# A fixed order and a window for the first loads of an encoder kernel, and tables loaded later

## The chip, the cores and the metric

The kernel runs on one core of a Trainium2 chip. The metric is the device time of one execution in microseconds; lower is better. The core has TensorE (PE, with its weight loads PEld), VectorE (DVE), ScalarE (ACT), GpSimd (POOL) and SyncE (SP). SP issues the loads here, and 16 DMA engines carry them out.

## The reference, cut to what matters

One encoder block in float32, 256 tokens of width 2048. The first projection of the input is where the change lies:

```
x (1, 256, 2048); w_in (2048, 2624)
proj = x @ w_in                       # split: q_a 1024, k_a 256, v_a 256, c_q 512, c_kv 512, k_r 64
q_a, k_a = rope(rms_norm(q_a, g_qa)), rope(rms_norm(k_a, g_ka))      # 8 and 2 heads of 128
o_a = attention(q_a, k_a, v_a)
q_b, kv_b = rms_norm(c_q, g_cq) @ w_uq, rms_norm(c_kv, g_ckv) @ w_ukv
o_b = attention(q_b with rope, kv_b and rope(k_r))
x = LN1(alpha*x + [o_a, o_b] @ w_out)
x = LN2(alpha*x + cross_attention(x, LNm(mem)))
x = LN3(alpha*x + relu(x @ w1)**2 @ w2)
```

## The kernel before

Every float32 matmul is made of three fast ones: a number is split into a rounded part (hi, an ACT copy to a rounded type) and a rest (lo, a DVE subtraction), and `mm3` multiplies hi by hi, hi by lo and lo by hi. `split` (lines 87 and 88) makes the two parts for inputs and weights alike.

Weights come through `Stream`. A stream reads tiles of up to 1 MB (128 partitions by 2048 numbers) into `raw`, of which there are three buffers, and hands out halves split into `w_hi` and `w_lo`. The load of a tile waits until the tile three before it has been split. The first group of queries, `q_group(0, prologue, 4)`, reads its four tiles finely (`fine=4`): each tile in four pieces of 512 columns, one piece for each k of the contraction (16 in all), at line 150. Ahead of each such piece `load_x` may load the part of the transposed input that this k needs (line 254): one k for k = 0 and 1, then two k together for each even k. So the program's order is x0, w0, x1, w1, x2 (for k = 2 and 3), w2, w3, x4, w4, w5, and so on. All other tiles are loaded whole, at line 152.

`proj_tokens` runs over k and, for each k, over the two blocks of 128 tokens: six matmuls for a k, adding up in two PSUM tiles `acc`. The streams in order are: w_qa's first four tiles (queries 0 to 3), w_ka (two tiles), w_vkr (four tiles of 640 KB), attention of four heads, then w_qa's other four tiles, then w_ckv and w_cq for the second attention. `qk_heads` normalizes and rotates the heads, with tables `tab` that POOL multiplies together at line 265.

Two helpers load small tables. `load_tables` (lines 258 to 260) loads the rotation tables and gains for q_a, k_a and k_r, and is called by `prologue` when k is 14, ahead of x14, w14 and w15. `load_more` (lines 268 to 271) loads the gains of the two latents, the rotation table for q_b and the rows for the later norms; the program has it between w_ka and w_vkr.

Before all this, `busy(8)` issues eight matmuls on a tile of ones.

The order of instructions on each engine is set by a planner when the program is built: it simulates a timeline and takes, on each engine, what is ready first by priority. It can thus move a load ahead of one that stands before it in the program. `queue` pins an order by hand: it adds an edge from each instruction given to it to the one before on the same engine. The stages of the MLP, far later, use it for PE, ACT and DVE. Loads are not pinned in the kernel before. Every load also uses one of a few semaphores in turn, and SP waits until the former load on that semaphore has landed.

Of the kernel before, what the change touches and what calls it, by code (L numbers as in the profile page):

```python
# [18 lines left out]
P = 128  # L19
S = 256  # L20
D = 2048
KT = D // P
# [16 lines left out]
def encoder_kernel(ctx: ExitStack, tc: tile.TileContext, t, out):  # L39
    nc = tc.nc  # L40
# [26 lines left out]
    def att_tile():  # L67
        return psT.tile([P, 512], F32, tag="att", name="att")

    def tmp_tile():  # L70
        return rings["tmp"].tile([P, 512], F32, tag="tmp", name="tmp")

    def lo_tile():
        if fixed_lo:
            fixed_lo.rotate(-1)
            return fixed_lo[-1]
        return rings["lo"].tile([P, 1024], F32R, tag="w_lo", name="w_lo")

    def raw_tile():
        return rawp.tile([P, 2048], F32, tag="raw", name="raw")  # L80
# [24 lines left out]
    def queue(ins):  # L105

        i = ins.ins
        if i.engine in queued:
            tc.add_manual_dep(i, queued[i.engine], mybir.DependencyInfo(
                mybir.DependencyClass.NoSync, mybir.DependencyReason.DATA), reason="queue")  # L110
        queued[i.engine] = i.name
        return ins

    def pump(n=1):

        for _ in range(n):
            if banks or side:
                (banks or side).popleft()()
# [4 lines left out]
    def busy(n):  # L123

        ps = acc_tile()
        for _ in range(n):
            tc.keep_in_program_order(
                nc.tensor.matmul(ps, ones, ones[:, None, :].broadcast_to([P, 4, P]),
                                 start=True, stop=True))

    busy(8)

    class Stream:


# [4 lines left out]
        def next(self, hi=None, lo=None):  # L140
            u, h = divmod(self.n, 2)
            size = self.ap.shape[2]
            w = size // 2
            if h == 0:
                self.raw = raw_tile()
            g = w // 2 if u < self.fine else w
            if u < self.fine:
                for i, o in enumerate(range(h * w, h * w + w, g)):
                    self.before(4 * u + 2 * h + i)
                    nc.sync.dma_start(self.raw[:, o:o + g], self.ap[u][:, o:o + g])  # L150
            elif h == 0:
                nc.sync.dma_start(self.raw[:, :size], self.ap[u])
            self.n += 1
            if hi is None:
                hi = wsp.tile([P, 1024], F32R, tag="w_hi", name="w_hi")
                lo = lo_tile()
            for o in range(0, w, g):
                self.split(hi[:, o:o + g], lo[:, o:o + g], self.raw[:, h * w + o:h * w + o + g],
                      pinned=self.pinned)
            pump(self.beside)  # L160
            return hi[:, :w], lo[:, :w]
# [7 lines left out]
    def proj_tokens(stream, xt, nk, cols, before=None, by_block=None, wide=None, tiles=None):  # L169


        ps = [(tiles or acc_tile)() for _ in range(NB + bool(by_block))]
        parts, k = [], 0
        while k < nk:
            if before is not None:
                before(k)
            hi, lo = stream.next() if wide is None else wide(k)
            kk = hi.shape[1] // cols
            hi = hi.rearrange("p (k c) -> p k c", c=cols)
            lo = lo.rearrange("p (k c) -> p k c", c=cols)  # L180
            parts.append([(k + j, hi[:, j, :], lo[:, j, :]) for j in range(kk)])
            k += kk
            if not by_block:
                tokens_mm(ps, xt, parts.pop(), nk, 0, cols, range(NB))
        if by_block:
            half = cols // 2
            pieces = [(0, 0, cols, ps[0]), (1, 0, half, ps[1]), (1, half, half, ps[2])]
            for b, c, w, p_ in pieces:
                for part in parts:
                    tokens_mm({b: p_}, xt, part, nk, c, w, [b])  # L190
        else:
            pieces = [(b, 0, cols, ps[b]) for b in range(NB)]
        return pieces if by_block is not None else ps

    def tokens_mm(ps, xt, part, nk, c, w, blocks):
        for k, hi, lo in part:
            for b in blocks:
                o = b * P
                mm3(ps[b][:, :w], xt[:, k, o:o + P], xt[:, k, S + o:S + o + P],
                    hi[:, c:c + w], lo[:, c:c + w], k == 0, k == nk - 1)  # L200
# [23 lines left out]
    def transpose_split(dst, src, k0, b, nk=4, width=P):  # L224

        ps = att_tile()
        for j in range(nk):
            nc.tensor.transpose(ps[:, j * P:(j + 1) * P], src[:, j * P:(j + 1) * P], ident)
        o = b * P
        v = ps[:, :nk * P].rearrange("p (k c) -> p k c", c=P)  # L230
        split(dst[:, k0:k0 + nk, o:o + P], dst[:, k0:k0 + nk, S + o:S + o + P], v)
# [4 lines left out]
    gcq, gckv = tab_a[:, 0:512], tab_a[:, 512:1024]  # L236
    tab = tab_a[:, 1024:2048].rearrange("p (i b c) -> p i b c", i=4, b=NB)
    cs_n, gr = tab_b[:, 0:512], tab_b[:, 512:1024]
    krt = tab_b[:, 1536:1792].rearrange("p (i b c) -> p i b c", i=2, b=NB)
    qrt = midp.tile([P, 2, S], F32, name="qrt")  # L240
    gbt = const.tile([P, 3, 2, KT], F32, name="gbt")
# [3 lines left out]
    xt = xt_t.rearrange("p (k c) -> p k c", c=512)  # L245
    x_raw = big.tile([P, 8192], F32, tag="big", name="x_raw")

    def load_x(k):

        n = 1 if k < 2 else 0 if k % 2 else 2  # L250
        if not n:
            return
        src = x_raw[:, k * S:(k + n) * S]
        nc.sync.dma_start(src, t["xT"][k // 4][:, (k % 4) * S:(k % 4 + n) * S])
        split(xt[:, k:k + n, 0:S], xt[:, k:k + n, S:2 * S], src.rearrange("p (k c) -> p k c", c=S))

    def load_tables():
        nc.sync.dma_start(cs_n, t["rope_a"])
        nc.sync.dma_start(gr, t["g_qk"].partition_broadcast(P))
        nc.sync.dma_start(krt, t["rope_kr"])  # L260
        for i in range(4):
            cs = cs_n[:, (i % 2) * 256:(i % 2) * 256 + 256].rearrange("p (b d) -> p b d", b=NB)
            g = gr[:, i * DH:(i + 1) * DH]
            for b in range(NB):
                nc.gpsimd.tensor_tensor(out=tab[:, i, b, :], in0=cs[:, b, :], in1=g, op=ALU.mult)

    def load_more():
        nc.sync.dma_start(gckv, t["g_ckv"].partition_broadcast(P))
        nc.sync.dma_start(gcq, t["g_cq"].partition_broadcast(P))
        nc.sync.dma_start(qrt, t["rope_qr"])  # L270
        nc.sync.dma_start(gbt, t["norm_rows"])

    attA = big.tile([P, 8192], F32R, tag="big", name="attA")
    qa = attA[:, 0:4096].rearrange("p (h c) -> p h c", c=512)
# [170 lines left out]
                  lambda st: (va[:, st, g * P:(g + 1) * P], va[:, st, 256 + g * P:256 + (g + 1) * P]),  # L445
                  ot, h)

    def q_group(g4, before=None, fine=0):
        stream = Stream(t["w_qa"][g4 * 4:g4 * 4 + 4], fine)
        stream.before = load_x  # L450
        ps = proj_tokens(stream, xt, KT, 512, before)
        for b in range(NB):
            qk_heads(ps[b], b, 4, tab[:, 0, b, :], tab[:, 1, b, :], qa, g4 * 4, SC_A)

    def prologue(k):
        if k == 14:
            load_tables()

    q_group(0, prologue, 4)
    ps = proj_tokens(Stream(t["w_ka"]), xt, KT, KVA * DH)  # L460
    for b in range(NB):
        qk_heads(ps[b], b, KVA, tab[:, 2, b, :], tab[:, 3, b, :], ka, 0)
    load_more()
    ps = proj_tokens(Stream(t["w_vkr"]), xt, KT, KVA * DH + ROPE)
    for b in range(NB):
        split(va[:, b, 0:256], va[:, b, 256:512], ps[b][:, 0:256])
        krn = tmp_tile()
        v = ps[b][:, 256:256 + ROPE]
        a, c, e = krn[:, 0:64], krn[:, 64:128], krn[:, 256:384]
        nc.vector.tensor_tensor(out=a, in0=v, in1=krt[:, 0, b, :], op=ALU.mult)  # L470
        for i in range(2):
            j = 1 - i
            nc.vector.tensor_tensor(out=c[:, i * 32:(i + 1) * 32], in0=v[:, j * 32:(j + 1) * 32],
                                    in1=krt[:, 1, b, i * 32:(i + 1) * 32], op=ALU.mult)
        nc.vector.tensor_tensor(
            out=e.rearrange("p (g c) -> p g c", g=2), in0=a[:, None, :].broadcast_to([P, 2, ROPE]),
            in1=c[:, None, :].broadcast_to([P, 2, ROPE]), op=ALU.add)
        transpose_split(kr, e, 0, b, nk=1)
    heads = Heads()
    for h in range(4):  # L480
        heads.step(gqa_head(h))
# [21 lines left out]
    for n in range(2):  # L503
        ps = proj_tokens(s_vb, ckv, RANK // P, 512)
# [186 lines left out]
    ps = proj_tokens(Stream(t["w_vm"]), memt, KT, 512)  # L691
# [18 lines left out]
    for n in range(2):  # L710
        ps = proj_tokens(s_om, om, HM, 512)
# [203 lines left out]
    for c, q in PASSES:  # L915
# [3 lines left out]
        for u in us:  # L919
            n = 2 if q == 0 and u[3] == (CH // 2 - 2 if c else 0) else 1  # L920
# [462 lines left out]
```

## Time and profile before

| what | value |
|---|---|
| median of 3 runs | 1097.58 us |
| lowest and highest run | 1096.8 and 1098.6 us |
| the profiled execution's own time | 1098.32 us |
| its span, first to last instruction | 1096.5 us |
| mean granted TensorE clock | 0.996 |
| TensorE busy | 1076.7 us (98%) |
| VectorE busy | 938.7 us (86%) |
| ScalarE busy | 642.3 us (59%) |
| mean DMA rate over the span | 197 GB/s |

The span is what the trace shows; the rest of the execution's time lies around it. In the rows below, L150 is line 150 of the kernel, PE acc L164 a matmul of that line into the tile acc, and `w_hi<-raw` means that w_hi is written from raw. "SPq" rows are loads issued by SP; their duration is that of the issue, not of the transfer. "x2" merges two neighbours of one kind. A bracket at the end of a row is the engine's idle time before it and what ended it.

### The profile page before, as it was taken

Reading aid. Unit: us, or ns where it says so; the run is one execution under the profiler, and the core shown is the slowest. Engines: PE = TensorE matmul, PEld = TensorE weight load, DVE = VectorE, ACT = ScalarE, POOL = GpSimd, SP = SyncE. Lnnn points to the kernel's source line nnn. Section 1 sums busy time; section 2 is a strip of 40 time slices with the busy share of each in tenths; the row PEclk is TensorE's granted clock in tenths of the full one; section 3 lists DMA queues with packets and bytes.
Section 4 is the critical chain, followed back from the end, with each engine's and each line's share of the span. In section 5 each row is a group of like instructions: output and inputs, shape, how many; then the busy total and the mean of one; then the engine's idle time right before and its main releaser. Section 6 shows DMA issues by size and latency. Waiting matters only on the chain.

```text
span 1096.5 us, 15253 instructions
## 1 busy us (share of the span) xinstructions
PE 1076.7 (98%) x5846; PEld 928.8 (85%) x5846; DVE 938.7 (86%) x1301; ACT 642.3 (59%) x937; POOL 36.2 (3%) x43
## 2 busy tenths in 40 slices
PE   9999999999999999999999999999999999999995
PEld 6988899988999878878888888888888888888885
DVE  6878678778889677999999999899999899999876
ACT  6555567555576426656566557466566566666640
POOL 2402000000000000000000000000000000000000
PEclk9999999999999999999999999999999999999998
DMA  9664454466577334555556555646556555655732
GB/s 327 246 227 136 156 189 157 156 228 238 182 216 267 143 128 176 209 192 198 191 202 244 202 188 199 216 170 226 198 186 225 198 192 198 224 175 195 253 145 78
DMA packets 37369, 215.87 MB, mean 197 GB/s; under 512 B 4272, under 2 KB 5168, under 8 KB 13616
## 3 DMA queue, kind: packets, MB, share of 16 engines
q1 hardware_dynamic: 37296, 214.89, 55.5%
q8 instruction: 46, 0.75, 0.3%
q14 instruction: 27, 0.22, 0.1%
HBM read 212.78 MB, written 2.10 MB: 196 GB/s over the span
## 4 chain that ended last, share of the span: by engine, by line
PE 92%; DVE 6%; issue 1%; ACT 1%; DMA 1%; SPq 0%; POOL 0%; DVEq 0%; ACTq 0%
PE acc L164 12%; PE acc L165 12%; PE acc L166 12%; PE acc L1035 11%; PE att L1035 6%; PE acc L1043 6%; PE att L165 5%; PE att L166 5%; PE att L164 5%; PE att L1043 3%; PE acc L206 2%; PE acc L204 2%; PE acc L205 2%; DVE lo L962 2%; PE acc L213 1%; PE att L213 1%
## 5 line engine op out<-in xcount | busy, mean ns | idle before, releaser
L87 ACT ACTIVATE w_hi<-raw 128x1024 fp32r<-128x1024 f32 (+2 forms) x134 | 131.6, 989 | 108.5 <-PE acc L166 73.9
L88 DVE TENSOR_TENSOR w_lo<-raw,w_hi 128x1024 fp32r<-128x1024 f32 (+2 forms) x130 | 147.2, 1142 | 50.3 <-ACT w_hi L87 49.2
L962 DVE TENSOR_TENSOR lo<-raw,w_hi 128x1024 fp32r<-128x1024 f32 (+1 forms) x156 | 173.0, 1128 | 9.2 <-ACT w_hi L961 9.0
L961 ACT ACTIVATE w_hi<-raw 128x1024 fp32r<-128x1024 f32 (+1 forms) x156 | 149.3, 980 | 25.5 <-PE acc L166 15.0
L1035 PE MATMUL acc<-x2t,w_hi 128*128 128x512 f32 x592 | 153.3, 391 | 0.0
L1035 PEld LDWEIGHTS acc<-x2t,w_hi 128*128 128x128 f32 x592 | 108.9, 189 | 19.6
L962 DVE TENSOR_TENSOR lo<-s_t,w_hi 128x1024 fp32r<-128x1024 f32 x84 | 102.4, 1222 | 10.8 <-ACT w_hi L961 10.7
L961 ACT ACTIVATE w_hi<-s_t 128x1024 fp32r<-128x1024 f32 x84 | 88.6, 1057 | 37.3 <-PE acc L1035 18.4
L1043 PEld LDWEIGHTS acc<-x2t,lo 128*128 128x128 f32 x592 | 80.8, 190 | 5.8
L1043 PE MATMUL acc<-x2t,lo 128*128 128x256 f32 x592 | 82.5, 282 | 0.0
L1035 PE MATMUL att<-x2t,w_hi 128*128 128x512 f32 x304 | 78.4, 391 | 0.0
L165 PE MATMUL acc<-lo,ht 128*128 128x512 f32 (+1 forms) x188 | 73.0, 389 | 1.1 <-DVE lo L962 1.1
L164 PE MATMUL acc<-w_hi,ht 128*128 128x512 f32 x186 | 72.5, 390 | 0.0
L166 PE MATMUL acc<-w_hi,ht 128*128 128x512 f32 x186 | 72.4, 389 | 0.0
L876 ACT ACTIVATE tmp<-acc 128x256 f32<-128x256 f32 x41 | 15.4, 384 | 92.2 <-PE acc L1035 87.9
L165 PE MATMUL acc<-w_lo,xt 128*128 128x512 f32 (+2 forms) x192 | 69.3, 362 | 0.0
L166 PE MATMUL acc<-w_hi,xt 128*128 128x512 f32 (+2 forms) x192 | 69.2, 361 | 0.0
L164 PE MATMUL acc<-w_hi,xt 128*128 128x512 f32 (+2 forms) x192 | 65.6, 361 | 1.2 <-ACT w_hi L87 1.2
L1035 PEld LDWEIGHTS att<-x2t,w_hi 128*128 128x128 f32 x304 | 55.8, 189 | 10.0
L962 DVE TENSOR_TENSOR lo<-raw_x,w_hi 128x1024 fp32r<-128x1024 f32 (+1 forms) x50 | 55.4, 1124 | 0.6 <-ACT w_hi L961 0.4
L165 PE MATMUL att<-lo,aux 128*128 128x512 f32 x139 | 54.4, 391 | 1.4 <-DVE lo L962 1.4
L164 PE MATMUL att<-w_hi,aux 128*128 128x512 f32 x139 | 54.1, 390 | 0.0
(287 smaller groups left out, 2513.1 us busy)
## 6 DMA issues: line engine op xcount, KB each, us to landing
raw<-in_w_mo SPq DMA_DIRECT2D x39, 1024.0 KB, 4.8
raw<-in_w_mc SPq DMA_DIRECT2D x37, 1024.0 KB, 4.8
raw<-in_w_out SPq DMA_DIRECT2D x16, 1024.0 KB, 4.9
raw_x<-in_w_mo SPq DMA_DIRECT2D x14, 1024.0 KB, 4.8
raw_x<-in_w_mc SPq DMA_DIRECT2D x12, 1024.0 KB, 4.8
row_b<-in_w_mo SPq DMA_DIRECT2D x11, 1024.0 KB, 4.8
raw<-in_w_mi SPq DMA_DIRECT2D x8, 1024.0 KB, 4.8
row_b<-in_w_mc SPq DMA_DIRECT2D x7, 1024.0 KB, 4.8
```

The costliest lines, as they stand in the source:

```text
L87: pin(nc.scalar.activation(hi, src, AF.Copy), pinned)
L88: return pin(nc.vector.tensor_tensor(out=lo, in0=src, in1=f(hi), op=ALU.subtract), pinned)
L164: keep(nc.tensor.matmul(ps, ah, bh, start=start, stop=False))
L165: keep(nc.tensor.matmul(ps, ah, bl, start=False, stop=False))
L166: keep(nc.tensor.matmul(ps, al, bh, start=False, stop=stop))
L204: nc.tensor.matmul(ps, hi, xt[:, k, 0:S], start=k == 0, stop=False)
L205: nc.tensor.matmul(ps, hi, xt[:, k, S:2 * S], start=False, stop=False)
L206: nc.tensor.matmul(ps, lo, xt[:, k, 0:S], start=False, stop=k == nk - 1)
L961: queue(nc.scalar.activation(hi, src, AF.Copy))
L962: queue(nc.vector.tensor_tensor(out=lo, in0=src, in1=f(hi), op=ALU.subtract))
L1035: queue(nc.tensor.matmul(ps, hi[:, k * P:(k + 1) * P], x2t[:, k0 + k, :], start=k0 + k == 0, stop=k0 + k == KT - 1))
L1043: queue(nc.tensor.matmul(ps[:, 0:S], lo[:, k * P:(k + 1) * P], x2t[:, k0 + k, 0:S], start=False, stop=False))
```

## The change

All loads of the first three streams go through a helper, `fetch_in_order`, which pins them on SP in the order of the program. In addition, each fine weight piece from the fourth on gets an edge with a semaphore to the piece three before it: SP issues it only when that one has landed. `load_tables` moves from ahead of x14 to behind the last fine piece, and `load_more` from between w_ka and w_vkr to behind w_vkr. The list `loads` is emptied after that, so later streams load as before.

```diff
+    loads = []
+
+    def fetch_in_order(dst, src):
+        return queue(nc.sync.dma_start(dst, src))
...
             if u < self.fine:
                 for i, o in enumerate(range(h * w, h * w + w, g)):
                     self.before(4 * u + 2 * h + i)
-                    nc.sync.dma_start(self.raw[:, o:o + g], self.ap[u][:, o:o + g])
+                    loads.append(fetch_in_order(self.raw[:, o:o + g], self.ap[u][:, o:o + g]).ins)
+                    if len(loads) > 3:
+                        tc.add_manual_dep(loads[-1], loads[-4].name, mybir.DependencyInfo(
+                            mybir.DependencyClass.Sync, mybir.DependencyReason.DATA), reason="turn")
             elif h == 0:
-                nc.sync.dma_start(self.raw[:, :size], self.ap[u])
+                (fetch_in_order if loads else nc.sync.dma_start)(self.raw[:, :size], self.ap[u])
...
-        nc.sync.dma_start(src, t["xT"][k // 4][:, (k % 4) * S:(k % 4 + n) * S])
+        fetch_in_order(src, t["xT"][k // 4][:, (k % 4) * S:(k % 4 + n) * S])
...
     def load_tables():
-        nc.sync.dma_start(cs_n, t["rope_a"])
+        fetch_in_order(cs_n, t["rope_a"])
...
-    def q_group(g4, before=None, fine=0):
+    def q_group(g4, fine=0):
         stream = Stream(t["w_qa"][g4 * 4:g4 * 4 + 4], fine)
         stream.before = load_x
-        ps = proj_tokens(stream, xt, KT, 512, before)
+        ps = proj_tokens(stream, xt, KT, 512)
+        if fine:
+            load_tables()
         for b in range(NB):
             qk_heads(ps[b], b, 4, tab[:, 0, b, :], tab[:, 1, b, :], qa, g4 * 4, SC_A)
 
-    def prologue(k):
-        if k == 14:
-            load_tables()
-
-    q_group(0, prologue, 4)
+    q_group(0, fine=4)
     ps = proj_tokens(Stream(t["w_ka"]), xt, KT, KVA * DH)
     for b in range(NB):
         qk_heads(ps[b], b, KVA, tab[:, 2, b, :], tab[:, 3, b, :], ka, 0)
-    load_more()
     ps = proj_tokens(Stream(t["w_vkr"]), xt, KT, KVA * DH + ROPE)
...
         transpose_split(kr, e, 0, b, nk=1)
+    load_more()
+    loads.clear()
     heads = Heads()
```

More of the change, by code (lines that the diff above doesn't have):

```diff
@@ L253, in load_x @@
         src = x_raw[:, k * S:(k + n) * S]
-        nc.sync.dma_start(src, t["xT"][k // 4][:, (k % 4) * S:(k % 4 + n) * S])
+        fetch_in_order(src, t["xT"][k // 4][:, (k % 4) * S:(k % 4 + n) * S])
         split(xt[:, k:k + n, 0:S], xt[:, k:k + n, S:2 * S], src.rearrange("p (k c) -> p k c", c=S))
     def load_tables():
-        nc.sync.dma_start(cs_n, t["rope_a"])
-        nc.sync.dma_start(gr, t["g_qk"].partition_broadcast(P))
-        nc.sync.dma_start(krt, t["rope_kr"])
+        fetch_in_order(cs_n, t["rope_a"])
+        fetch_in_order(gr, t["g_qk"].partition_broadcast(P))
+        fetch_in_order(krt, t["rope_kr"])
         for i in range(4):
@@ L267, in load_more @@
     def load_more():
[L268 to L271, printed above, removed]
+        fetch_in_order(gckv, t["g_ckv"].partition_broadcast(P))
+        fetch_in_order(gcq, t["g_cq"].partition_broadcast(P))
+        fetch_in_order(qrt, t["rope_qr"])
+        fetch_in_order(gbt, t["norm_rows"])
     attA = big.tile([P, 8192], F32R, tag="big", name="attA")
```

## The prediction

> **What bounds the kernel now.** I read the page first (span, busy times, the chain that ended last), then the windows of the span, then the waits, the chain and the timeline of the first 30 us, since the diff touches only loads issued there.
>
> ```profile
> span 1096.5 us, 15253 instructions
> PE 1076.7 (98%) x5846; PEld 928.8 (85%) x5846; DVE 938.7 (86%) x1301; ACT 642.3 (59%) x937; POOL 36.2 (3%) x43
> ...
> PE 92%; DVE 6%; issue 1%; ACT 1%; DMA 1%; SPq 0%; POOL 0%; DVEq 0%; ACTq 0%
> ```
>
> TensorE bounds it: 98% busy, and 92% of the chain. A change to loads can only win where PE waits for a load. The windows (first column the stretch, then each engine's busy us) tell where that can be:
>
> ```profile
> core 0: us, PE busy (x) PEld busy (x) DVE busy (x) ACT busy (x) POOL busy (x), PEclk, DMA share, GB/s
> 5.00:12.00 7.00, 6.12 (x21) 3.56 (x22) 4.65 (x8) 4.35 (x8) 0.00 (x0) 1.00 0.92 331
> 12.00:30.00 18.00, 18.00 (x85) 15.04 (x84) 14.11 (x20) 12.78 (x20) 4.77 (x8) 1.00 1.04 385
> 30.00:60.00 30.00, 30.00 (x217) 29.30 (x216) 25.59 (x52) 15.87 (x23) 12.00 (x8) 1.00 0.67 228
> ...
> 390.00:402.00 12.00, 9.72 (x53) 7.50 (x53) 8.69 (x21) 2.15 (x4) 0.54 (x1) 0.86 0.00 0
> ...
> 465.00:585.00 120.00, 115.89 (x580) 96.39 (x580) 114.92 (x140) 73.67 (x95) 0.00 (x0) 1.00 0.56 199
> ```
>
> From 12 to 60 us PE has no hole, though the DMA engines are as full as they get until 30. The holes behind the start lie at 390 to 402 (2.3 us) and 465 to 585 (4.1 us), where no touched load runs. So the field of the change is the first 12 us. There the chain and the timeline say:
>
> ```profile
> 3.06 5.94 DMA raw<-in_w_qa
> 9.03 0.64 ACT w_hi L87
> 9.71 0.73 PE acc L164 x2
> ...
> 11.62 0.45 PE acc L164 x2
> ...
> 12.98 0.45 PE acc L164 x2
> ```
> ```profile
> 8.48 0.39 PE L166 MATMUL acc<-w_hi,xt 128*128 128x512 f32 x1
> ...
> 9.71 0.50 PE L164 MATMUL acc<-w_hi,xt 128*128 128x512 f32 x1 [0.84 <-ACT w_hi L87]
> ```
> ```profile
> PE acc L164 <- ACT w_hi L87: 1.2, 2, 0.8
> ```
>
> The chain enters through the third weight load (w2; I number the sixteen 256 KB pieces w0 to w15, and an x load by the k it starts with): issued at 3.06, landed at 9.00, rounded by ACT, first matmul at 9.71. One k (six matmuls) takes 12.98 - 11.62 = 1.36 us, 0.23 a matmul. The matmul before began at 8.48, so PE could have begun k2 at 8.71: it lost 9.71 - 8.71 = 1.0 us. The two waits of PE for w_hi in these 12 us are 1.2 us together; the other, before k1, is for w1. All that earlier loads can give is thus about 1.2 us, of which w2 holds 1.0.
>
> **The change, part by part.** What SP issues now:
>
> ```profile
> 0.74 0.38 SPq L254 DMA_DIRECT2D x_raw<-in_xT  x1
> 1.17 0.42 SPq L150 DMA_DIRECT2D raw<-in_w_qa  x1
> ...
> 2.11 0.43 SPq L150 DMA_DIRECT2D raw<-in_w_qa  x1
> 2.58 0.43 SPq L254 DMA_DIRECT2D x_raw<-in_xT  x1
> 3.06 0.91 SPq L150 DMA_DIRECT2D raw<-in_w_qa  x2
> 4.01 0.43 SPq L254 DMA_DIRECT2D x_raw<-in_xT  x1
> 4.48 0.91 SPq L150 DMA_DIRECT2D raw<-in_w_qa  x2
> ...
> 11.08 0.33 SPq L254 DMA_DIRECT2D x_raw<-in_xT  x1
> ...
> 13.08 0.33 SPq L254 DMA_DIRECT2D x_raw<-in_xT  x1
> ...
> 15.13 0.33 SPq L258 DMA_DIRECT2D tab_b<-in_rope_a  x1
> ...
> 22.25 0.33 SPq L152 DMA_DIRECT2D raw<-in_w_ka  x1
> 25.34 13.31 SPq L152 DMA_DIRECT2D raw<-in_w_vkr  x4
> 43.18 12.22 SPq L152 DMA_DIRECT2D raw<-in_w_qa  x4
> ```
>
> *The fixed order.* x0, w0, x1, w1, x2, w2, w3, x4, w4, w5: that is already the program's order, so for the x and weight pieces pinning it moves nothing: 0 us, no other end.
>
> *The waits.* Thirteen weight loads (w3 to w15) now wait for the landing of the third weight load ahead. The landing times, issue to landing, from four single issues (0.74, 1.17, 2.11, 3.06) and from all of 6 to 24 us:
>
> ```profile
> x_raw<-in_xT SPq DMA_DIRECT2D x1, 128.0 KB, 2.1
> ```
> ```profile
> raw<-in_w_qa SPq DMA_DIRECT2D x1, 256.0 KB, 3.2
> ```
> ```profile
> raw<-in_w_qa SPq DMA_DIRECT2D x1, 256.0 KB, 4.1
> ```
> ```profile
> raw<-in_w_qa SPq DMA_DIRECT2D x1, 256.0 KB, 5.9
> ```
> ```profile
> raw<-in_w_qa SPq DMA_DIRECT2D x10, 256.0 KB, 5.4
> ```
>
> w0 lands at 4.3, w1 at 6.2, w2 at 9.0. So w3 is issued at about 4.35 (3.5 now), x4 behind it at 4.8, w4 at 6.3 (4.5 now), w5 at 9.0 or when w2 lands (5.0 now), and x6 queued behind w5 on SP. Does the pipe run empty? Three loads are issued in 13.08 - 11.08 = 2.0 us, so in the full state one lands each 0.67 us, and 5.4 us is eight of them: the 5.4 is queueing, not a price of a load. With the wait, when w(i-3) lands there stand behind it two weight loads and one or two x loads: three or four, 2.0 to 2.7 us of transfer. A new load needs at most 2.1 - 0.3 = 1.8 us from issue to its first byte (the lone x0: 2.1 us, less 128 KB at the full rate). 1.8 is below 2.0, so the slowest DMA engine still has work when the next load arrives, and every landing from w3 on stays where it is: cost 0. At w2 the margin is thinnest: w3, x4, w4 (2.0 us) stand behind it when w5 is issued. Ends: 0, and +4.6 if a load took 5.4 us even with a short queue (rival 2). I take 0, since a round of 1.8 us plus queue is nearest to the 3.2 us row, and PE needs three weights only each 3 x 1.36 = 4.08 us.
>
> *What the waits may give.* Two windows show an odd thing: many loads are queued from 3 us on, yet the DMA engines move far less before 8 us than after 9.
>
> ```profile
> 2.00:8.00 6.00, 5.61 (x16) 2.20 (x15) 2.52 (x5) 2.63 (x6) 0.00 (x0) 1.00 0.80 260
> 9.00:24.00 15.00, 14.29 (x62) 11.56 (x63) 12.30 (x19) 12.26 (x20) 2.71 (x6) 1.00 1.05 381
> ```
>
> If later loads slow w2's last part, holding back w3, w4, w5 and x6 brings w2 forward. Earliest: behind w1 (6.2) come x2 and w2 at 0.67 us each, so w2 not before 7.5, and PE then gains the whole 1.0. Latest: nothing new stands ahead of w2 on the queue, so 9.0 and a gain of 0; a loss is excluded by the same reason. Between: only w3 (0.8 us later), w4 and w5 leave the scene before 8 us, x4 and w3 remain, and 260 GB/s is not the full rate, so contention for bandwidth can't be the whole story. I take 0.3 us, nearer to 0. The Trainium skill (DMA: Bandwidth & Descriptors, Queues, rings and completion order) says that on each DMA engine the descriptors of one queue are consumed in ring order; by that, w3 to w5 can never delay w2, and the gain would be 0 (rival 1). The steady 0.67 us between landings agrees with it; the slow first 8 us it does not explain.
>
> *Tables.* load_tables (rope_a, g_qk, rope_kr: 256 + 256 + 128 KB) moves from ahead of x14, w14, w15 to behind them: these three come 640/256 x 0.67 = 1.7 us earlier, PE had no hole there (gain 0), and the same bytes stand ahead of the first w_ka load (cost 0). g_qk, now behind three more loads, lands 3 x 0.67 = 2.0 us later, so POOL's products move from 21.3 to about 23.3 and end at about 28.1; their first reader on DVE is at 30.1, so 2.0 us of cover remain.
>
> ```profile
> 21.29 4.77 POOL L265 TENSOR_TENSOR tab_a<-tab_b 128x128 f32<-128x128 f32 x8 [19.98 <-DMA tab_b<-in_g_qk]
> ```
> ```profile
> 30.12 0.68 DVE L311 TENSOR_TENSOR tmp<-acc,tab_a 128x512 f32<-128x512 f32 x1
> ```
> ```profile
> 123.53 0.74 DVE L290 SCALAR_TENSOR_TENSOR tmp<-acc,rs_r,tab_a 128x512 f32<-128x512 f32 x1
> ```
>
> If the cover went, each us beyond it would be one us of DVE, then PE. load_more's four loads (3 x 256 + 48 KB, 2.1 us of transfer) move past the second w_ka and all four w_vkr loads, to behind the last one. w_ka's second load lands that much earlier (no PE hole: gain 0). On SP the four issues, 0.33 us each and at most 2.7 us at the 0.67 us pitch, fit between the last w_vkr issue (25.34 + 13.31 = 38.65) and the next weight load at 43.18, which waits for a free buffer: cost 0; uncovered, that load would come up to 2.1 us later. Their first reader, g_ckv in L290, is at 123.5.
>
> Sum: -0.3 (w2) + 0 + 0 + 0 on the profiled execution's 1098.3 gives 1098.0; that execution stands 0.7 above the median of the three runs, so against 1097.6 the sum is 1097.3. About 0.2% (2.2 us) is what a measurement of this kernel can tell from no change, and the ceiling of 1.2 us lies below that.
>
> **The rivals.** *1. The wait does nothing for w2* (ring order, or the slow first 8 us have another cause): 1097.6. For it: queued loads don't saturate the DMA engines then. Against: w2's 5.9 us is longer than any load's ahead of it.
>
> *2. Slower: the round trip starves PE.* The chain w3, w6, w9, w12, w15 has four rounds from 9.7 us (w3's landing now, 0.67 behind w2). At 5.4 us a round w15 lands at 31.3 and k15 starts 0.7 later, at 32.0, where it now starts at 9.71 + 13 x 1.36 = 27.4: +4.6, 1102.2. It costs from a round of (27.4 - 0.7 - 9.7) / 4 = 4.25 us on and passes 2.2 us at 4.8. For it: w2 took 5.9 with only five loads ahead of it, so short queues don't guarantee short rounds early on. Against: w0's 3.2, and that 5.4 is exactly eight landings. The Trainium skill (DMA: Bandwidth & Descriptors, Anatomy of one DMA) gives a fit, for another issuing path, of 2.0 us plus bytes at 436 GB/s, by estimate 2.6 us for such a load, which would be well below 4.25.
>
> *3. The planner.* Instructions not pinned by hand are ordered by a simulated timeline; new edges early shift it, and ACT, DVE and PE may get another order as far as 400 us. For it: DVE is busy 25.59 of 30 us from 30 to 60, so one misplaced split is a hole of one to two us. Two or three such make +2.5 to +4: 1100 to 1101.6. To the other side, an order that closes part of the 2.3 and 4.1 us holes named above: -2.3 to -4, 1093.6 to 1095.3. Against both: what would be reordered is hidden, and the later order is written by hand.
>
> **How the numbers follow.** Forecast (w2 a little earlier) 0.45; rival 1 0.36; rival 2 0.05; rival 3 slower 0.08, faster 0.06. The first two are both within 0.2%: same 0.81, slower 0.13, faster 0.06. Their own range is 1096.4 (the ceiling of 1.2 off 1097.6) to 1098.6, the highest run before. The range 1095.5 to 1100.5 reaches into rival 3 on both sides and leaves out rival 2, most of rival 3's slower end and its faster end, about 0.15.
>
> **What would show it.** Right: SP issues w3 near 4.3, w4 near 6.3, w5 at w2's landing; the DMA rate from 9 to 24 us stays near 380 GB/s; weight loads land some 3 us after issue instead of 5.4; PE's hole before k2 is 0.7 us instead of 1.0, and there is none from 12 to 60; POOL's products start near 23 and end before 30; w_ka's second load lands before 30. Wrong: a hole of PE at each third k (rival 2), the DMA rate at 300 or less there, or new waits of PE on w_lo between 30 and 400 us with another order of instructions (rival 3).

## The result: slower by 0.62%, and the profile after

The changed kernel takes 1104.39 us (median of 6 runs, 1103.26 to 1105.63) against 1097.49 us before (6 runs): ratio 1.0062, 95% interval 1.0049 to 1.0075, that is 5.4 to 8.2 us. The forecast was no change, 1097.3, with 1100.5 as its upper end. The profiled execution of the changed kernel took 1104.01 us, its span is 5.7 us longer than before.

From the page of the changed kernel, the span, TensorE's row and the chain that ended last:

```profile
span 1102.2 us, 15260 instructions
PE 1077.8 (98%) x5846; PEld 929.5 (84%) x5846; DVE 938.8 (85%) x1301; ACT 641.9 (58%) x937; POOL 33.3 (3%) x43
...
PE 89%; DVE 6%; DMA 3%; issue 1%; ACT 1%; SPq 0%; POOL 0%; DVEq 0%; ACTq 0%
```

PE's work is the same; 3% of the chain is now DMA where it was 1%. The windows show where (same columns as before: stretch, busy us of each engine, granted clock, DMA share, GB/s):

```profile
5.00:12.00 7.00, 6.20 (x26) 4.73 (x26) 5.13 (x8) 5.34 (x9) 0.00 (x0) 1.00 0.93 300
12.00:30.00 18.00, 17.15 (x72) 12.75 (x70) 10.74 (x16) 9.43 (x16) 0.71 (x2) 1.00 0.82 264
30.00:60.00 30.00, 25.80 (x181) 25.49 (x182) 22.30 (x40) 13.99 (x21) 13.15 (x15) 0.89 0.68 238
```
```profile
2.00:8.00 6.00, 4.85 (x15) 2.15 (x14) 2.65 (x5) 3.15 (x7) 0.00 (x0) 1.00 0.84 279
9.00:24.00 15.00, 14.76 (x63) 11.07 (x61) 10.12 (x16) 10.09 (x17) 0.00 (x0) 1.00 0.87 271
...
29.00:39.00 10.00, 5.18 (x23) 4.50 (x22) 5.28 (x8) 4.87 (x6) 4.33 (x9) 0.66 0.77 305
```

Two numbers matter. From 9 to 24 us the DMA engines move 271 GB/s, where they moved 381. And from 29 to 39 us PE is busy for only 5.18 of 10 us, at a mean clock of 0.66. The timeline of PE, its waits up to 60 us and the chain show what it waits for there:

```profile
29.00 0.39 PE L174 MATMUL acc<-w_hi,xt 128*128 128x512 f32 x1
33.74 0.80 PE L172 MATMUL acc<-w_hi,xt 128*128 128x256 f32 x2 [4.36 <-ACT w_hi L87]
35.00 0.58 PE L173 MATMUL acc<-w_lo,xt 128*128 128x256 f32 x1 [0.46 <-DVE w_lo L88]
```
```profile
PE acc L172 <- ACT w_hi L87: 5.7, 3, 4.4
```
```profile
24.46 8.07 DMA raw<-in_w_ka
...
32.63 1.06 ACT w_hi L87
...
33.72 1.24 DVE w_lo L88
...
35.00 0.58 PE acc L173
35.59 0.21 PE acc L174
35.80 0.21 PE acc L173
```

The last matmul of the first group starts at 29.0. The next one needs the first w_ka tile, which lands at 24.46 + 8.07 = 32.5 us. Before, the tile was issued at 19.17, landed 6.9 us later, at 26.0, and its first matmul followed the first group at 29.14 without a pause:

```profile
19.17 0.33 SPq L152 DMA_DIRECT2D raw<-in_w_ka  x1
```
```profile
raw<-in_w_ka SPq DMA_DIRECT2D x1, 1024.0 KB, 6.9
```
```profile
29.14 0.40 PE L164 MATMUL acc<-w_hi,xt 128*128 128x256 f32 x2
```

Changed, PE stands still for 4.5 us (counted from when its next matmul could have started), waits again for the rest (w_lo), and then runs a 256-column matmul each 0.21 us instead of 0.12 until 38.9: its clock is at half after the hole. Adding up, over all neighbouring matmuls, how far their starts lie apart beyond the usual 0.227 us (512 columns) and 0.120 us (256 columns): before, PE lost 3.1 us from 4.3 to 12 us and nothing from there to 60. Changed, it loses 2.0 us up to 12 us, 1.2 from 12 to 28 and 7.3 from 28 to 42: 7.4 us more in all.

Comparing the 5846 matmuls one by one gives the same: from 45 to 385 us each runs 7.4 us later than before, from 410 us to the last one 6.0 to 6.1. So no later stage loses anything. The 1.4 us that come back near 400 us are chance: in the profile before, the clock was at half from 397.3 to 400.7 us (0.86 in 390 to 402), and in this one it was not. With 0.4 us less after the last matmul, that leaves the 5.7 us by which the profiled spans differ.

SP's queue shows why the tile was late:

```profile
6.19 1.60 SPq L136 DMA_DIRECT2D raw<-in_w_qa  x2
...
9.10 1.85 SPq L136 DMA_DIRECT2D raw<-in_w_qa  x2
...
11.47 1.57 SPq L136 DMA_DIRECT2D raw<-in_w_qa  x2
...
14.55 1.70 SPq L136 DMA_DIRECT2D raw<-in_w_qa  x2
...
16.82 1.39 SPq L136 DMA_DIRECT2D raw<-in_w_qa  x2
...
20.96 2.02 SPq L136 DMA_DIRECT2D raw<-in_w_qa  x2
23.02 0.43 SPq L136 DMA_DIRECT2D tab_b<-in_rope_a  x1
...
24.46 0.91 SPq L136 DMA_DIRECT2D raw<-in_w_ka  x2
```

Each pair of weight pieces, with its x load, goes out 2.95 us after the one before ((20.96 - 6.19) / 5); in the full state before it was 2.0 us. PE uses up a pair in 2.72 us. So the stream that was faster than PE by a third is now slower than PE. The tables and w_ka stand behind it.

### The profile page after: what moved, and what is told of

It is laid out like the page before. It is cut to its first block, busy times and chain, and to the rows that moved or that the text cites. A ratio compares the mean times of both kernels' runs of the same rounds, so it can differ in the third digit from the quotient of the medians.

```text
span 1102.2 us, 15260 instructions
## 1 busy us (share of the span) xinstructions
PE 1077.8 (98%) x5846; PEld 929.5 (84%) x5846; DVE 938.8 (85%) x1301; ACT 641.9 (58%) x937; POOL 33.3 (3%) x43
## 4 chain that ended last, share of the span: by engine, by line
PE 89%; DVE 6%; DMA 3%; issue 1%; ACT 1%; SPq 0%; POOL 0%; DVEq 0%; ACTq 0%
PE acc L173 12%; PE acc L172 11%; PE acc L174 11%; PE acc L1042 11%; PE att L1042 6%; PE acc L1050 6%; PE att L173 5%; PE att L174 5%; PE att L172 5%; PE att L1050 3%; PE acc L214 2%; PE acc L212 2%; PE acc L213 2%; DVE lo L969 2%; DMA raw<-in_w_qa 1%; PE acc L221 1%
## 5 line engine op out<-in xcount | busy, mean ns | idle before, releaser
L968 ACT ACTIVATE w_hi<-raw 128x1024 fp32r<-128x1024 f32 (+1 forms) x156 | 149.3, 980 | 25.6 <-PE acc L174 13.4
```

The lines of the kernel that those rows point to most:

```text
L968: queue(nc.scalar.activation(hi, src, AF.Copy))
```

## The experiments

Landing times below are those of one profiled execution of each kernel. They scatter: w0 is issued at 1.2 us behind the same load in all kernels with 256 KB pieces, and lands between 4.3 and 5.1.

Theory A: the window of three leaves too little in flight, the DMA engines run partly empty, and w_ka, behind the stream, comes late. Theory B: the pinned order, or the tables between w15 and w_ka, hold w_ka back.

**No waits.** The pins and the later tables stay:

```diff
-                    if len(loads) > 3:
-                        tc.add_manual_dep(loads[-1], loads[-4].name, ...)
```

> The changed kernel without the thirteen waits; the pinned order and the later tables stay. Theory A (the window of three starves the DMA engines): weight piece w15 lands near 22 us instead of 26.2, the first w_ka load near 26 instead of 32.5, PE's 4.5 us hole before w_ka is gone, the DMA rate from 9 to 24 us is back near 380 GB/s; time 1097.5, within 1096.5 to 1098.6. Theory B (the tables, now between w15 and w_ka, or the pinned order hold w_ka back): the hole stays at 3 us or more, time 1101 to 1104.

Measured: 1097.95 us, ratio to before 1.0004 (0.9994 to 1.0013). The window from 9 to 24 us:

```profile
9.00:24.00 15.00, 15.00 (x66) 11.96 (x65) 13.31 (x20) 12.03 (x20) 0.93 (x3) 1.00 1.05 389
```

w15 lands at 21.6 us and w_ka at 27.3 (issue plus time to landing). Taking the waits out takes the whole slowdown out. Pins and later tables together cost nothing that the times can tell, so theory B falls as the cause, and with it the rival of the planner. In the profiled execution PE is 0.5 us behind the kernel before from 45 us on: w_ka lands 1.3 us later than there, and PE waits 0.7 us for its w_lo. Whether that is chance the one trace does not show.

**A window of six.** `len(loads) > 6` and `loads[-7]`.

> Each fine weight load waits for the sixth ahead of it instead of the third. Theory A: with six weight loads and three x loads allowed in flight the queue is as deep as before the change, w15 lands before 24 us, no hole of PE; time 1097 to 1099. Theory B (tables or pins): as the changed kernel, 1101 to 1104.

Measured: 1097.11 us, ratio 0.9994 (0.9984 to 1.0004); the waits are in the program, and nothing is lost:

```profile
9.00:24.00 15.00, 14.22 (x61) 11.48 (x62) 13.26 (x20) 12.49 (x20) 0.31 (x1) 1.00 1.04 373
```

But this window hardly ever holds a load back. The loads use eight semaphores in turn, so that even without added waits no more than eight are in flight, and six weight pieces with their three x loads make nine. From 9 to 16 us the traces have 8.0 loads in flight (issued and not yet landed) here, 8.0 without waits, 8.0 before, and 4.5 in the changed kernel. So this run shows only that a wait which is already over costs nothing; whether the depth is the cause, windows of two and four have to tell.

**Waits, with the tables at their old places.** `prologue` with `load_tables` at k = 14 and `load_more` ahead of w_vkr, as before the change; waits and pins stay.

> The waits and the pinned order, with both groups of tables back at their places of before. Theory A: the DMA engines lose as much in the window, so the first w_ka load still lands near 31 to 33 us and PE's hole moves or stays, 4 to 5 us in all (part of it before k14, whose loads come 1.7 us later); time 1102 to 1105. Theory B: 1097 to 1099.

Measured: 1103.15 us, ratio 1.005 (1.0034 to 1.0066). The hole splits, as theory A has it: PE waits 2.2 us before k14 (from 26.1 us) and again for w_ka. Its waits up to 60 us:

```profile
PE acc L172 <- ACT w_hi L87: 3.0, 3, 2.0
```

The kernel is slow with the tables in either place, so their move is not the cause.

**Waits, without the table loads.**

```diff
     def load_tables():
-        fetch_in_order(cs_n, t["rope_a"])
-        fetch_in_order(gr, t["g_qk"].partition_broadcast(P))
-        fetch_in_order(krt, t["rope_kr"])
+        nc.gpsimd.memset(tab_b, 1.0)
```

> The changed kernel with the three loads of load_tables left out; the tables are filled with ones on POOL, so the rotation and gains of q_a and k_a are not applied. 640 KB fewer stand between w15 and w_ka. Theory A: w15 lands late as in the changed kernel (26 us), w_ka about 3 us sooner than there (29 instead of 32.5), the hole falls from 4.5 to 1 to 2 us; time 1100 to 1102. Theory B: w_ka lands near 26 and the hole is gone, 1097 to 1098.

Measured: 1100.68 us, ratio 1.0025 (1.0015 to 1.0034). The waits for w_hi fall from 5.7 to 2.8 us:

```profile
PE acc L172 <- ACT w_hi L87: 2.8, 3, 1.4
```

w_ka lands at 30.8, 1.7 us sooner. That this is just what 640 KB take at the full rate is luck: w15 lands 2.2 us later than in the changed kernel (28.4 instead of 26.2, with fifteen of its sixteen parts there by 25.7), and w_ka then 2.4 us behind it instead of 6.3. By the ratios the table loads ahead of w_ka cost some 4 us once the stream is late. What remains above the kernel before (2.7 us) is put down to the window, as the only change left that the runs found to cost anything.

**Windows of two and four.** `len(loads) > 2` with `loads[-3]`, and `len(loads) > 4` with `loads[-5]`. Theory A1: the rate goes with what is in flight. Theory A2: each wait costs a fixed gap.

> Each fine weight load waits for the second ahead of it instead of the third. Theory A1 (the pipe runs empty: a round from issue to landing takes some 4 us whatever the depth, so the rate goes with the number of loads in flight): rounds of about 4 us for two weight loads, so w15 lands at 7 rounds x 4 + 6 = 34 us instead of 26, the rate from 9 to 24 us is 180 GB/s, and PE starves already inside the first group; time 1111 to 1115. Theory A2 (each wait costs a fixed gap on SP or the queue, whatever the depth): fourteen waits instead of thirteen, time 1104 to 1106.

> Each fine weight load waits for the fourth ahead of it. Theory A1: four weight loads and two x loads in flight in a round of 4 to 4.5 us, 1.5 MB or about 350 GB/s, close to the full 385; the first w_ka load lands at 27 to 29 us and PE's hole is 0 to 1.5 us; time 1097.5 to 1099.5. Theory A2 (a fixed gap for each wait): twelve waits instead of thirteen, time 1103 to 1105.

Measured: 1107.61 us for two (ratio 1.0093, 1.008 to 1.0106) and 1099.07 for four (1.001, 1.0 to 1.0019). Their windows from 9 to 24 us, two and then four, and the loads issued there with a window of two:

```profile
9.00:24.00 15.00, 14.20 (x53) 8.78 (x52) 8.09 (x13) 8.22 (x13) 0.00 (x0) 1.00 0.69 222
```
```profile
9.00:24.00 15.00, 15.00 (x66) 12.39 (x65) 12.40 (x19) 11.67 (x19) 0.00 (x0) 1.00 0.96 324
```
```profile
raw<-in_w_qa SPq DMA_DIRECT2D x9, 256.0 KB, 3.5
```

A2 falls: fourteen, thirteen, twelve and ten waits (windows of two, three, four and six) cost 10, 7, 1 and 0 us. A1 holds: the rate goes with what is in flight. But I had put a window of two at 1111 to 1115: with less in flight the round also gets shorter, 3.5 us from issue to landing instead of 4.

| window, in weight pieces | in flight, 9 to 16 us: loads, MB | GB/s, 9 to 24 us | DMA share | first w_ka tile lands, us | median, us | ratio to before, same series |
|---|---|---|---|---|---|---|
| 2 | 3.1, 0.8 | 222 | 0.69 | 36.8 | 1107.61 | 1.0093 |
| 3 (the change) | 4.5, 1.1 | 271 | 0.87 | 32.5 | 1104.39 | 1.0062 |
| 4 | 6.1, 1.5 | 324 | 0.96 | 28.5 | 1099.07 | 1.0010 |
| 6 | 8.0, 2.0 | 373 | 1.04 | 26.6 | 1097.11 | 0.9994 |
| none, pins and later tables | 8.0, 2.0 | 389 | 1.05 | 27.3 | 1097.95 | 1.0004 |
| before | 8.0, 2.0 | 381 | 1.05 | 26.0 | 1097.49 | |

Medians of different series differ by up to 1 us for the same kernel (before: 1097.5 to 1098.5), so windows are compared by the ratio.

**The same window in larger pieces.** Still three weight loads, but of 512 KB:

```diff
-            g = w // 2 if u < self.fine else w
+            g = w
...
-                    self.before(4 * u + 2 * h + i)
+                    self.before(4 * u + 2 * h)
+                    self.before(4 * u + 2 * h + 1)
```

> The changed kernel with fine pieces of 1024 columns (512 KB, two k each) instead of 512: the window is still three weight loads, but 1.5 MB of weights instead of 0.75. Theory A1 (bytes in flight set the rate): the pipe stays full, 9 to 24 us near 370 GB/s, w_ka near 27, no hole there beyond 1 us; the first matmul comes 0.7 to 1 us later since the first piece is larger; time 1098 to 1099.5. Rival (what counts is the number of loads or waits in flight, not bytes): rate near 265, w_ka at 30 or later, 1102 to 1105.

Measured: 1102.55 us, ratio 1.0035 (1.0021 to 1.0049). The rate is back, and w_ka lands at 26.5 with no hole after it.

```profile
9.00:24.00 15.00, 14.96 (x59) 11.79 (x58) 13.14 (x15) 10.57 (x13) 0.29 (x1) 1.00 1.02 370
```
```profile
8.38 1.22 PE L173 MATMUL acc<-w_hi,xt 128*128 128x512 f32 x2 [3.73 <-ACT w_hi L87]
```

The window is the same in weight loads, but each of them now has an x load beside it. So the total rises too: from 9 to 16 us 6.2 loads and 2.3 MB are in flight, where the changed kernel has 4.5 loads and 1.1 MB. The fair partner is the window of four, with 6.1 loads and 1.5 MB: at the same number of loads, 9 to 16 us shows 389 GB/s here and 338 there. That leaves bytes in flight, not loads or waits. The packets of the larger pieces (4 KB, median 159 ns, against 2 KB in 84 ns) explain at most 6% of these 15%.

The time I missed: the first piece lands at 7.3 instead of 4.3 us, so PE starts at 8.4 instead of 5.0, and its clock, at half since the start, stays there until 13 us.

**Waits on w3, w4 and w5 alone**, with the tables as changed and with the tables at their old places: `if 3 < len(loads) < 7`. The changed kernel had shown w2 landing at 7.5 us where it landed at 9.0, and PE's hole before k2 gone.

> Only w3, w4 and w5 wait for the third weight load ahead; w6 to w15 don't. Theory A1: w2 lands near 7.5 us as in the changed kernel (9.0 before), so PE's 1.0 us hole before k2 is gone, and from w6 on the queue fills up and the rate is full; w_ka lands near 26 to 27, no hole there; time 1096.4 to 1097.2, the fastest so far. Rival (the early landing of w2 is chance, not the waits): w2 at 8.5 to 9.0, 1097 to 1098. Theory A2: three gaps, 1098 to 1099.

> As the one with waits on w3, w4 and w5 alone, but with both groups of tables at their places of before, so that the three small table loads stand ahead of x14 and not just ahead of w_ka. Theory A1: w2 near 7.5, first w_ka load near 26; 1096.3 to 1097.0. Rival (chance): 1097 to 1098.

Measured: 1099.54 us (ratio 1.0016, 1.0007 to 1.0024) and 1099.63 (1.0014, 1.0006 to 1.0023): slower than before, and my expectation is missed. w2 lands at 7.5 in both, so its early landing is no chance. But w5, which waits for w2, comes 1.7 to 2.0 us after w4 instead of 0.67, and most of that gap is still in the stream at w15: against the kernels with the same order and no waits, w15 lands 1.3 us later (22.8, 21.6) and 1.1 us later (24.6, 23.6). w_ka lands at 28.2 and 29.1, which is 0.9 and 3.1 us later; where the 2 us more of the second come from is not shown. With the tables as changed, PE's waits up to 60 us and its window around w_ka:

```profile
PE acc L172 <- ACT w_hi L87: 1.4, 2, 0.9
...
PE acc L173 <- DVE w_lo L88: 0.8, 1, 0.8
```
```profile
28.00:36.00 8.00, 6.34 (x36) 5.72 (x35) 6.57 (x12) 5.60 (x7) 1.71 (x2) 0.79 0.48 179
```

This gave theory C: up to the first w_ka tile the whole start is one DMA stream with about as much in it as PE has work, so what PE wins at k2 it gives back at w_ka unless the stream gets shorter too.

**The first w_ka tile ahead of the tables**, with waits on w3 to w5, with none, and with one on w3:

```diff
+        def fetch_first(self):
+            self.raw, self.fetched = raw_tile(), 0
+            fetch_in_order(self.raw[:, :self.ap.shape[2]], self.ap[0])
...
         if fine:
+            s_ka.fetch_first()
             load_tables()
```

> Waits on w3, w4, w5 alone, and the first w_ka tile loaded ahead of the three table loads (they stand between the two w_ka tiles). Theory C (until the first w_ka tile PE is bound by the DMA stream: what is lost in it is paid before w_ka, what is taken out of it is won there): w_ka lands 640 KB or 1.7 us sooner than with waits on three and tables ahead, at about 26.5, its hole of 1.1 and 0.9 us is gone, the gain before k2 is kept; 1096.3 to 1097.3. Rival: the tables, now later, hold the heads of the first group (POOL's products end at about 33 instead of 29), 1098 to 1100.

> No waits, and the first w_ka tile ahead of the three table loads. Theory C: w_ka lands near 24.5; PE has no hole there and none to fill, so only w2's stay at 8.5 to 9.0 counts: 1097 to 1098, as without waits and with tables ahead. Rival (tables late): 1098 to 1100.

> Only w3 waits (for w0), and the first w_ka tile stands ahead of the table loads. Theory C: if it is w3's late issue that brings w2 forward, w2 lands near 7.5, the pipe loses nothing after it, w_ka near 25, no hole at either place: 1096.2 to 1097.0. If it takes the waits of w4 and w5 too, w2 lands at 8.5 to 9.0 and the time is 1097 to 1098.

Measured: three waits 1097.97 us (ratio 0.9994, 0.9985 to 1.0002); none 1097.92 (0.9995, 0.9986 to 1.0004); one wait 1097.29 (0.9996, 0.9987 to 1.0005). None can be told from before, or from each other. What the traces show agrees with theory C: w_ka lands at 25.6, 24.5 and 24.6 us, there is no hole behind it in any of the three, and the later tables (POOL's products from 27.7 with three waits) hold nobody up: its window around w_ka is full.

```profile
28.00:36.00 8.00, 8.00 (x63) 7.64 (x62) 7.99 (x12) 4.46 (x6) 7.83 (x11) 1.00 0.55 197
```

With one wait w2 lands at 7.7, and PE goes on without a hole before k2 (8.81):

```profile
7.71 0.63 ACT L87 ACTIVATE w_hi<-raw 128x512 fp32r<-128x512 f32 x1
```
```profile
8.57 0.40 PE L181 MATMUL acc<-w_hi,xt 128*128 128x512 f32 x1
8.81 0.62 PE L179 MATMUL acc<-w_hi,xt 128*128 128x512 f32 x2
```

But w4 then lands at 11.3 instead of 11.1 and PE waits 0.5 us there, so of the 1.0 us 0.4 is left: counted as above, PE loses 2.7 us from 4.3 to 28 where before lost 3.1, and from 45 us on its matmuls run 0.4 us earlier than before. With three waits even that was eaten by the clock: PE's matmuls came each 0.43 us, not 0.23, until 8.9 us, and from 45 us on they run as late as before.

```profile
7.05 0.63 PE L180 MATMUL acc<-w_lo,xt 128*128 128x512 f32 x1
7.48 0.63 PE L181 MATMUL acc<-w_hi,xt 128*128 128x512 f32 x1
...
9.29 0.39 PE L180 MATMUL acc<-w_lo,xt 128*128 128x512 f32 x1
9.53 0.39 PE L181 MATMUL acc<-w_hi,xt 128*128 128x512 f32 x1
```

## Why the prediction was wrong, step by step

*What bounds the kernel.* Right as far as it went: PE bounds it, and of the first 60 us only the first 12 had holes. The conclusion "so the field of the change is the first 12 us" was wrong. That there is no hole says that nothing is late, but not how much later it may come. The DMA engines were full until 30 us, and the loads landed only a little ahead of their use: w_ka landed at 26.0 and its first matmul ran at 29.1. That distance was the number to work out.

*The fixed order, 0 us.* Right: pinned order and later tables without waits, 1.0004.

*The waits' cost, 0 us: the step that failed.* I said that when a weight load lands, 2.0 to 2.7 us of transfer stand behind it, a new load needs 1.8 us to its first byte, so the slowest DMA engine never runs dry. The round from issue to landing would have been about 3.0 us, a pair of weights each 2.0 us. Measured: 3.9 us for the fine pieces from 5 to 23 us,

```profile
raw<-in_w_qa SPq DMA_DIRECT2D x13, 256.0 KB, 3.9
```

and a pair each 2.95 us. The sign that I had named for being wrong, a DMA rate of 300 GB/s or less from 9 to 24 us, came with 271.

Two things were wrong in the step. The 1.8 us was read off the lone first load of 128 KB; in the window of two, with one or two loads ahead of it, a 256 KB piece still takes 3.5 us. And I asked only whether the slowest engine still has work. A load counts as landed when the last of its sixteen parts is done: in the changed kernel those of w6 end between 11.66 and 12.69 us, and SP issues w9, which waits for w6, at 12.71. By then the engines that were done first stand idle. That is shown: from 9 to 24 us fewer than sixteen packets are under way, so that at least one engine is idle, during 5% of the time before, never without waits, and during 66% of it in the changed kernel, with only six of them at 11.8 us, where w6 ends and w7 has hardly begun. Why one part lags behind the others, and whether it is always the same engine's, is not shown, since the trace doesn't name the engine of a packet. The Trainium skill (DMA: Bandwidth & Descriptors, Anatomy of one DMA) has a fit of 2.0 us plus the bytes at 436 GB/s, by estimate 2.6 us for such a piece; it speaks of another issuing path, and the 3.5 us here is longer. The measurement decides.

*Rival 2* had the right cause, with a chance of 0.05, and the wrong place. I asked whether k15's weight would be late, and got 4.25 us as the round from which it costs. w3 landed at 9.1 and w15 at 26.2, four rounds of 4.3 us: just that bound, and k15 hardly waited. What was late was the load behind it. Against the same order without waits, the stream lay behind by 4.7 us at w15 (26.2, 21.6) and by 5.2 at w_ka (32.5, 27.3); against the kernel before, w_ka came 6.5 us later. The price is then not what PE lacks in the group, but all that the stream has lost by w_ka less its distance of about 2 us (from 26.0 to 29.1, less 1.1 us of ACT for w_hi): 4.5 us of hole, and what the clock adds to it.

*What the waits may give, 0.3 us.* Too low: w2 landed at 7.45, the earliest I had allowed, and the hole before k2 went wholly (1.7 us lost from 7.5 to 12 before, 0.0 changed); at 14 us PE was 1.1 us ahead of before. In the seven kernels where w3 waits for w0, w2 lands between 7.45 and 7.7; in the four with 256 KB pieces where no load waits that early, between 8.5 and 9.2 (8.1 with the window of four, where w4 is the one to wait for w0, and 7.4 with the window of two, where w2 itself waits). So rival 1 falls too. The rule of the Trainium skill behind it (DMA: Bandwidth & Descriptors, Queues, rings and completion order) says in which order an engine takes up the descriptors of its ring, and adds that a later one may finish its write before an earlier one. That a later load can't delay an earlier one does not follow from it, and the runs show the contrary. By what path the later loads delay it they do not show.

*Tables, 0 us.* Right by themselves: without the waits POOL's products start at 23.1, where I had put them at 23.3. In the changed kernel POOL's products started at 29.3, not 23.3, since the tables came behind the late stream; their first reader on DVE came later too, at 36.6, behind the late w_ka.

*Rival 3.* Nothing of it was seen: with the pins and without the waits the kernel is as fast as before, and in the changed kernel the 7.4 us stay the same from 45 to 385 us.

## What to carry to other kernels

A stage without a hole on the bound engine can still have a stream with no reserve: before a change to the order or the depth of loads, write down for each load how long before its first use it lands, for the load behind the changed ones too. A window on loads is to be measured in bytes in flight against the rate: here it took eight loads of 256 KB, 2 MB, for the full 380 GB/s, and the kernel before had just these, since its loads share eight semaphores. And a gain at one hole is worth nothing until the next load on the same path is early as well.

## What the runs showed of the hardware that I had not expected

The DMA rate with the depth, in the table above: 222, 271, 324, 373 and 389 GB/s. It is not only idle time; in the change the busy share fell by 17% (1.05 to 0.87) but the bytes by 29% (381 to 271), so packets took longer as well. Not the usual packet: the median of the 2 KB packets is 84 ns in both. The mean rose from 90 to 104 ns through a few long ones: 90 of 1988 took over 200 ns, before 38 of 2372. Why they are more stays open, as does the low rate of the first 8 us, 250 to 301 GB/s in every kernel here.

PE's clock: the 4.5 us hole was followed by half clock until 38.9 us, which made it dearer by some 2 us. The Trainium skill (TensorE: Matmul & The Clock Gate, Part 1: The HAM clock gate) says that TensorE goes to half rate after about 3.4 us of idling, judged in a window that runs freely. The hole of the change agrees. But with waits on w3 to w5 the clock fell to half as well (0.79 in 28 to 36 us) after holes of only 1.1 and 0.9 us close together, while the window of four kept full clock through 0.4 and 0.9 us. So shorter holes can be enough; a threshold the runs do not give.

The traces do show the window's grid: in all fourteen the clock's changes lie whole multiples of 3.413 us apart (in the changed kernel full for 27.307 us, then half for 6.827, that is eight times and twice). Where that grid lies differs from one execution to the next. So the clock came up at 4.7 us before and at 8.9 with three waits and w_ka first, for much the same matmuls. That alone cost the latter some 0.9 us (PE lost 2.8 us up to 12 us, and 1.9 with one wait), about as much as the whole gain in question.
